# A fourth pair of weight tiles, another order of the seven steps, and other ranks in the feed-forward of a hybrid encoder

## The chip, the cores and the metric

The kernel runs on one core of a Trainium2 chip. The metric is the device time of one execution in microseconds (us). A core has five engines that run side by side, each with its own stream of instructions in a fixed order: TensorE (PE in the profile; PEld is its weight load), VectorE (DVE), ScalarE (ACT), GpSimd (POOL) and SyncE (SP). An engine that waits at one instruction runs none of those behind it. [...]

## What is computed

544 tokens (512 of a new stream, 32 of a running one) go through two layers of width 1024. Around the mixers (Mamba-2 in layer 0, stick-breaking attention in layer 1) stand four SwiGLU feed-forwards of 2816 hidden columns, and these are what the change touches:

```python
def swiglu(h, w_gate, w_up, w_down):
    return (jax.nn.silu(h @ w_gate) * (h @ w_up)) @ w_down
...
x = x + 0.5 * swiglu(rms_norm(x, ffn_norm[i, 0]), ffn_w_gate[i, 0], ffn_w_up[i, 0], ffn_w_down[i, 0])
...        # mixer
x = x + 0.5 * swiglu(rms_norm(x, ffn_norm[i, 1]), ffn_w_gate[i, 1], ffn_w_up[i, 1], ffn_w_down[i, 1])
```

## The kernel before

The stream x lies transposed in the core's memory, 1024 features as 8 blocks c of 128 partitions, with all T = 544 tokens as columns; H = 272 is half of them. Every product is made of three matmuls in a rounded format: a value is taken apart into a high part and the rest (`xh`, `xl` for data, `whi`, `wlo` for weights), and hi·hi, hi·lo and lo·hi are added. So each weight tile that arrives by DMA must be converted before PE can use it: `whi<-...` on ACT or POOL, then `wlo<-...` on DVE or POOL (`halve`). The converted pairs are the scarce store: `NW = 3` pairs in turn, and the conversion for the step after next can only start when PE has left a pair.

One feed-forward (class `Sevens`, called four times, FF0 to FF3 below) runs its 22 blocks f of 128 hidden columns so:

- f = 0 to 3 are plain: gate and up product, 8 blocks c each (`product`).
- The other 18 go as nine pairs, x0 to x8, each by a Strassen-Winograd scheme of seven steps (`STEPS`): a11, s3, s2, a12, s1, a22, s4. Here a11, a12, a22 are quarters of the weight matrix, s3 and s1 are sums of two quarters, s2 is s3 plus a22, and s4 is s2 plus a12. A step is 24 matmuls of 272 columns on one weight pair. Sums of x's parts (`xfh`, `xfl`) are made once per feed-forward.
- The hidden values of a group of pairs are multiplied by the down weights by the same seven steps, twice per group (for two halves of the outputs): h0 and h0' after x1, h1 and h1' after x4, h2 and h2' after x7. A step is 18 matmuls, on `h3h`/`h4h` parts; its result is added to x by DVE (`add`: `x<-mm,x`). Four last products d0 to d3 close the feed-forward.

A sum such as s3 comes by two DMAs: SP fetches one quarter into the tile `s`, then POOL issues a second that adds the other quarter (`added`). There is one s3 tile: the next pair's s3 is fetched when the last one's is converted and s2 has been formed from it.

What sets the order of instructions on an engine is a planner (class `Plan`). Chains of work ask for time on an engine, for a slot ("get", "put") or for an event ("wait", "set"); each chain has a rank, and of those ready the lowest rank goes first. DMAs stand in it as fixed sleeps:

```python
            def added(self, key, tag, name):
                yield "sleep", 4.5
                yield "D", 1.0, lambda: G.dma_start(self.raw[key, tag][:, :self.width(key)], self.quarter_of(key, name), accum_op=ALU.add)
                yield "sleep", 5.0
                yield "set", ("raw", key, tag)
```

The conversions have rank 10, `add` and the copies of banks (`save`, `quarter`) 20, and `plain`, which turns the two banks of a plain f into hidden values, has the rank of the chain that starts it. The steps of x0 and of all h groups run in the order (0, 3, 2, 1, 4, 5, 6) of `STEPS`, those of x1 to x8 in the order 0 to 6. A plain f, and a pair's product, goes into one of four places in PSUM (`mm`), which PE can fill again only when ACT or DVE has read it.

Of the kernel before, what the change touches and what calls it, by code (L numbers as in the profile page):

```python
# [9 lines left out]
P = 128  # L10
# [171 lines left out]
def _body(tc, io):  # L182
# [22 lines left out]
    with ExitStack() as ctx:  # L205
# [3 lines left out]
        def halves(ap):  # L209
            return ap.rearrange("p (a b) -> p a b", a=2)  # L210

        xg = {}

# [138 lines left out]
        class Norm:  # L352
            def __init__(self, name, ring=None, share=None):
                self.g = NORMS[name]
                self.name = name
                self.ring = ring
                self.share = share
                self.parts = [None] * KC
                self.acc = None

            def ops(self, c):
                h, l = self.place(c)
                gp = gains[:, self.g, c:c + 1]
                yield "S", s_cost(T), lambda: S.activation(h, x[c], AF.Identity, scale=gp)
                yield "V", v_cost(T) + 0.06, lambda: V.scalar_tensor_tensor(out=l, in0=x[c], scalar=gp, in1=h.bitcast(F32), op0=ALU.mult, op1=ALU.subtract)
# [68 lines left out]
        def opening(norm, psum, tmp):  # L434
# [17 lines left out]
            def block(c):  # L452
                h, l = norm.place(c)
                gp = gains[:, norm.g, c:c + 1]
                S.activation(h, x[c], AF.Identity, scale=gp)
                V.scalar_tensor_tensor(out=l, in0=x[c], scalar=gp, in1=h.bitcast(F32), op0=ALU.mult, op1=ALU.subtract)

# [96 lines left out]
        STEPS = (("a11", "A", "b11"), ("s3", "D", 1), ("s2", "A", 2), ("a12", "B", "b21"), ("s1", "A", 0), ("a22", "D", 3), ("s4", "A", "b22"))  # L554

        class Sevens:

            NW = 3

            def __init__(self, plan, i, norm, bank, tmp, hidden, roles, after, first=(), opened=None, ahead=None, done=None):  # L560
# [5 lines left out]
                self.forms = Forms(norm)  # L566
                self.hs, self.hf, self.loaded, self.raw, self.gu = {}, {}, {}, {}, {}
# [62 lines left out]
            def weights(self):  # L630
                raw, tmp = self.raw, self.tmp
                for k, u in enumerate(self.units):
                    n, free = 1024, None
                    if k < len(self.first):
                        yield "get", "w"
                        self.loaded[k] = self.first[k]
                        yield "set", ("part", k)
                        continue
# [27 lines left out]

                    third = k % self.NW == 2
                    if third and k >= len(self.units) - self.NW:
                        yield "get", "w"
                        third = False  # L670
                    yield "get", "w"
                    if third:
                        hi, lo = (tmp.tile([P, 1024], F32R, tag=t, name=t) for t in ("whi", "wlo"))
                    else:
                        hi, lo = weight_parts()
                    self.loaded[k] = hi, lo
                    yield "spawn", self.halve(k, n, src, hi, lo, free), -2 if k == 0 and self.opened else 10
# [19 lines left out]
            def dense(self):  # L697
                banks = {}
                for k, u in enumerate(self.units):
# [3 lines left out]
                    if u[0] == "s":  # L703
# [16 lines left out]
                        for c in range(n):  # L720
# [31 lines left out]
                    elif u[0] == "p":  # L752
# [7 lines left out]
                        for c in range(KC - (late and j == 0)):  # L760
                            if late and j == 1 and c == 2:
                                yield "T", 0.753, lambda: product(banks[f, 0], self.loaded[k - 1], self.norm.parts, only=KC - 1)
                                yield "put", "w"
                                yield "set", "f0"
                            yield "T", 0.753, lambda: product(ps, self.loaded[k], self.norm.parts, only=c)
                        if not late or j == 1:
                            yield "put", "w"
                        if j == 1:
                            yield "spawn", self.plain(f, banks[f, 0], ps, self.plain_banks[f % 2])
                    else:  # L770
# [3 lines left out]
                        for at, (m, e) in enumerate(order):  # L774
# [7 lines left out]
                            if e == n - 1:  # L782
                                yield "spawn", self.leave(m, ps, f"b{b}"), 9
                        yield "put", "w"
# [94 lines left out]

            def united(self, p, u, w, s, t, *slots):  # L880

# [12 lines left out]
                yield "V", v_cost(H) + 0.06, lambda: V.scalar_tensor_tensor(out=s3, in0=s2, scalar=-1.0, in1=w0, op0=ALU.mult, op1=ALU.subtract)  # L894
                yield from self.apart(h3[:, 1:3, :], l3[:, 1:3, :], w, T)
                yield "set", ("hf", p, "b21")
                yield "set", ("hf", p, "b22")
# [7 lines left out]
            def plain(self, f, pg, pu, banks):  # L905
# [1347 lines left out]
```

## Time and profile before

| | |
|---|---|
| median of 3 runs | 2251.42 us (2250.7 to 2253.66) |
| profiled execution, its own time | 2249.7 us |
| its span, first to last instruction | 2247.8 us |
| granted TensorE clock | 0.995 of full speed |
| PE busy | 2204.1 us (98%), 17505 matmuls |
| DVE busy | 1827.7 us (81%), 2491 instructions |
| ACT busy | 1098.8 us (49%) |
| POOL busy | 597.6 us (27%) |
| DMA | 319 MB, 142 GB/s on average |

Stages, read from the timeline: FF0 to 380 us, Mamba to 804, FF1 to 1162, an embedding stage and the keys and values to 1250, FF2 to 1615, attention to 1806, FF3 to 2170, the rest to 2248. In the profile every operation has line 194, that of a recording helper, so groups are told apart by the names of their tiles. The duration of a POOL DMA row (0.9 us) is the issue alone; the landing is given by the DMA views.

### The profile page before, as it was taken

To read this page: it belongs to the slowest core of one execution; us is meant where nothing else is said; L and a number is where in the kernel's file an instruction comes from. 1 tells how busy PE (TensorE), PEld (TensorE's weight loads), DVE (VectorE), ACT (ScalarE), POOL (GpSimd) and SP (SyncE) were. 2 spreads that over 40 slices of the span, in tenths; PEclk is the share of its full clock that TensorE was granted. 3 is DMA by queue.
4 is the path that set the end of the run, shared out by engine and by line. 5 is a ranking of instruction groups with operands and counts; after the bars stand their busy time and mean duration, and the time that the engine had idled before them with its cause. 6 is when DMAs were issued, how large, how long until landed. Compare 5 with 4: busy or idle time off the path is not lost. (4 is left out here: it accounts for less than half of the span.)

```text
span 2247.8 us, 42746 instructions
## 1 busy us (share of the span) xinstructions
PE 2204.1 (98%) x17505; PEld 2152.0 (96%) x17505; DVE 1827.7 (81%) x2491; ACT 1098.8 (49%) x1585; POOL 597.6 (27%) x622
## 2 busy tenths in 40 slices
PE   9999999999999999999999999999998999999997
PEld 9999999999999999999999999999986899999997
DVE  7889887778877688898867788988788688898867
ACT  5434434567746454344345443443557254344353
POOL 2221321254323112222210223222234322222204
PEclk9999999999999999999999999999999999999999
DMA  6576862332333255868632658686311156868622
GB/s 211 139 205 165 218 161 76 113 113 92 108 108 95 92 160 140 216 167 207 160 94 85 200 141 209 171 208 159 100 47 49 53 167 148 214 167 202 158 86 78
DMA packets 117955, 319.23 MB, mean 142 GB/s; under 512 B 15200, under 2 KB 36320, under 8 KB 117760
## 3 DMA queue, kind: packets, MB, share of 16 engines
q1 hardware_dynamic: 91760, 233.23, 32.1%
q0 software_dynamic: 23120, 77.74, 19.3%
q10 hardware_dynamic: 2880, 5.53, 0.7%
q8 instruction: 138, 2.26, 0.4%
q14 instruction: 57, 0.47, 0.1%
HBM read 309.75 MB, written 6.71 MB: 141 GB/s over the span
## 5 line engine op out<-in xcount | busy, mean ns | idle before, releaser
L194 PE MATMUL mm<-xh,whi 128*128 128x272 f32 x2096 | 512.9, 292 | 5.8 <-DVE sq L194 3.8
L194 PE MATMUL mm<-xl,whi 128*128 128x272 f32 x2096 | 506.4, 289 | 0.3 <-DVE xl L194 0.3
L194 PE MATMUL mm<-xh,wlo 128*128 128x272 f32 x2096 | 505.1, 289 | 0.5 <-DVE wlo L194 0.5
L194 ACT ACTIVATE whi<-s 128x1024 fp32r<-128x1024 f32 (+1 forms) x196 | 190.5, 972 | 409.5 <-PE mm L194 291.8
L194 PEld LDWEIGHTS mm<-xh,whi 128*128 128x128 f32 x2096 | 357.0, 188 | 16.5 <-issue 13.9
L194 PEld LDWEIGHTS mm<-xh,wlo 128*128 128x128 f32 x2096 | 357.6, 189 | 0.7 <-DVE wlo L194 0.7
L194 PEld LDWEIGHTS mm<-xl,whi 128*128 128x128 f32 x2096 | 357.2, 189 | 0.5 <-DVE xl L194 0.5
L194 PE MATMUL mm<-xfh,wlo 128*128 128x272 f32 x1152 | 333.0, 289 | 9.3 <-DVE wlo L194 9.3
L194 PE MATMUL mm<-xfh,whi 128*128 128x272 f32 x1152 | 332.6, 289 | 1.0 <-ACT whi L194 0.9
L194 PE MATMUL mm<-xfl,whi 128*128 128x272 f32 x1152 | 331.7, 288 | 0.0
L194 DVE TENSOR_TENSOR wlo<-s,whi 128x1024 fp32r<-128x1024 f32 (+1 forms) x240 | 275.4, 1148 | 37.8 <-ACT whi L194 26.1
L194 ACT ACTIVATE whi<-a 128x1024 fp32r<-128x1024 f32 (+1 forms) x154 | 152.6, 991 | 221.0 <-PE mm L194 165.8
L194 DVE TENSOR_TENSOR wlo<-wraw,whi 128x1024 fp32r<-128x1024 f32 (+2 forms) x146 | 181.9, 1247 | 62.1 <-ACT whi L194 44.6
L194 DVE TENSOR_TENSOR wlo<-a,whi 128x1024 fp32r<-128x1024 f32 (+1 forms) x181 | 204.0, 1127 | 30.2 <-ACT whi L194 22.6
L194 PEld LDWEIGHTS mm<-xfh,wlo 128*128 128x128 f32 x1152 | 216.6, 188 | 12.0 <-DVE wlo L194 12.0
L194 PE MATMUL mm<-h4h,wlo 128*128 128x272 f32 x832 | 219.3, 289 | 1.8 <-DVE wlo L194 1.8
L194 PE MATMUL mm<-h4h,whi 128*128 128x272 f32 x832 | 219.3, 289 | 1.6 <-DVE x L194 1.5
L194 PEld LDWEIGHTS mm<-xfh,whi 128*128 128x128 f32 x1152 | 216.6, 188 | 2.6 <-ACT whi L194 2.3
L194 PE MATMUL mm<-h4l,whi 128*128 128x272 f32 x832 | 218.9, 288 | 0.0
L194 PEld LDWEIGHTS mm<-xfl,whi 128*128 128x128 f32 x1152 | 216.7, 188 | 0.0
L194 ACT ACTIVATE whi<-wraw 128x1024 fp32r<-128x1024 f32 (+2 forms) x116 | 119.8, 1034 | 172.9 <-PE mm L194 105.2
L194 POOL DMA_DIRECT2D s<-in_wgq x108 | 95.1, 881 | 353.7 <-DMA s<-in_wgq 146.4
(322 smaller groups left out, 4982.6 us busy)
## 6 DMA issues: line engine op xcount, KB each, us to landing
a<-in_wgq SPq DMA_DIRECT2D x108, 512.0 KB, 5.9
s<-in_wgq POOLq DMA_DIRECT2D x108, 512.0 KB, 7.4
s<-in_wgq SPq DMA_DIRECT2D x72, 512.0 KB, 4.4
a<-in_wd SPq DMA_DIRECT2D x72, 384.0 KB, 4.5
wraw<-in_win SPq DMA_DIRECT2D x41, 512.0 KB, 3.6
s<-in_wd SPq DMA_DIRECT2D x48, 384.0 KB, 3.1
s<-in_wd POOLq DMA_DIRECT2D x48, 384.0 KB, 7.3
wraw<-in_wgu SPq DMA_DIRECT2D x29, 512.0 KB, 3.7
```

The costliest lines, as they stand in the source:

```text
L194: ins = getattr(self.engine, op)(*args, **kw)
```

## The change

1. **Fourth weight pair.** x's parts for c < 4 now lie in two tiles of [128, 2, 4, 272] (class `Apart`), so that half 1 of all four, which only the plain products read, is one piece of 1088 columns. After the last plain product it serves as a fourth pair, until the last step of x8. It has the name of the part it lies in, so a conversion into it reads `xh<-...` and `xl<-...` in the rows. Pairs are handed out in the order in which PE leaves them. The writes of these parts are now 128x2x272 in form, formerly 128x544.
2. **Order of steps.** In x1 to x8, a22 is now the fourth step and a12 the sixth. The second half of each hidden group (h0', h1', h2') takes s3 as its second step (formerly the fourth), and a22 as its fourth.
3. **Ranks.** `add` goes from 20 to 9, ahead of the conversions; `plain` gets 4; a slot of the last plain pair is freed earlier.

```diff
+        class Apart:
+            def __init__(self, tile, c):
+                self.whole = tile[:, :, c, :]
+
+            def __getitem__(self, key):
+                a, start = divmod(key[1].start, H)
+                return self.whole[:, a, start:start + key[1].stop - key[1].start]
...
-                yield "S", s_cost(T), lambda: S.activation(h, x[c], AF.Identity, scale=gp)
+                yield "S", s_cost(T), lambda: S.activation(whole(h), halves(x[c]), AF.Identity, scale=gp)
...
-                    self.parts[c] = tuple(xg["pool"].tile([P, T], F32R, tag=f"x{k}{c}", name=f"x{k}{c}") for k in "hl")
+                    if c < 4 and not self.near:
+                        self.near = [xg["pool"].tile([P, 2, 4, H], F32R, tag=f"x{k}", name=f"x{k}") for k in "hl"]
+                    self.parts[c] = tuple(Apart(v, c) for v in self.near) if c < 4 else \
+                        tuple(xg["pool"].tile([P, T], F32R, tag=f"x{k}{c}", name=f"x{k}{c}") for k in "hl")
...
+        LATE, SOON = (0, 3, 2, 1, 4, 5, 6), (0, 1, 2, 5, 4, 3, 6)
...
+                self.places = ["pool", "pool", "tmp"]
...
-                    self.units += [("s", ("x", p), s) for s in ((0, 3, 2, 1, 4, 5, 6) if p == 0 else range(7))]
+                    self.units += [("s", ("x", p), s) for s in (LATE if p == 0 else SOON)]
...
-                            self.units += [("s", ("h", g, a), s) for a in range(2) for s in (0, 3, 2, 1, 4, 5, 6)]
+                            self.units += [("s", ("h", g, a), s) for a in range(2) for s in (SOON if a else LATE)]
...
-                    third = k % self.NW == 2
-                    if third and k >= len(self.units) - self.NW:
+                    yield "get", "w"
+                    place = self.places.pop(0)
+                    while place == "tmp" and k >= len(self.units) - self.NW or place == "x" and k > self.last_step:
                         yield "get", "w"
-                        third = False
-                    yield "get", "w"
-                    if third:
+                        place = self.places.pop(0)
+                    if place == "tmp":
                         hi, lo = (tmp.tile([P, 1024], F32R, tag=t, name=t) for t in ("whi", "wlo"))
+                    elif place == "x":
+                        hi, lo = (v[:, 1, :, :].rearrange("p c n -> p (c n)")[:, :1024] for v in self.norm.near)
...
-                        yield "put", "w"
+                        yield from self.leave_w(k)
                         if hidden:
-                            yield "spawn", self.add(it, s, ps, f"b{b}" if s in (3, 5, 6) else None), 20
+                            yield "spawn", self.add(it, s, ps, f"b{b}" if s in (3, 5, 6) else None), 9
...
+                        if (f, j) == (NPLAIN - 1, 1):
+                            self.places.append("x")
                             yield "put", "w"
                         if j == 1:
-                            yield "spawn", self.plain(f, banks[f, 0], ps, self.plain_banks[f % 2])
+                            yield "spawn", self.plain(f, banks[f, 0], ps, self.plain_banks[f % 2]), 4
...
+            def leave_w(self, k):
+                self.places.append(self.placed[k])
+                yield "put", "w"
...
-                    yield from self.united(f // 2, a, b, s, t, "sq", "acc")
-                    yield "put", "sq"
-                    yield "put", "c2"
+                    yield from self.united(f // 2, a, b, s, t, "sq", "acc", early=("c2", "sq"))
```

The planner then writes another order for the whole program. PE has as many matmuls as before, SP as many DMAs. POOL multiplies gate by up (`gu<-gu`) 6 times instead of 24, DVE does the rest, and POOL makes 10 of the `wlo` instead of 1.

**Place 1: h1' and x5 in FF1.** DVE before, from the conversion of h1' a11 on; `s3_11679` is the s3 of h1', `s3_11859` that of x5, `x2_67<-mm` an addition to x:

```order
L194 TENSOR_TENSOR wlo_11762<-a11_11584,whi_11761 128x768
L194 SCALAR_TENSOR_TENSOR x2_67<-mm_11709,x2_67 128x2x272
L194 TENSOR_TENSOR wlo_11787<-a12_11724,whi_11786 128x768
L194 TENSOR_TENSOR s2_11803<-s3_11679,a22_11744 128x768
L194 SCALAR_TENSOR_TENSOR x0_65<-mm_11629,x0_65 128x2x272
L194 TENSOR_TENSOR wlo_11819<-s2_11803,whi_11818 128x768
L194 SCALAR_TENSOR_TENSOR x1_66<-mm_11811,x1_66 128x2x272
L194 TENSOR_TENSOR wlo_11836<-s3_11679,whi_11835 128x768
```

DVE now, from the same conversion on; `s3_11573` is the s3 of h1':

```order
L194 TENSOR_TENSOR wlo_11643<-a11_11459,whi_11642 128x768
L194 SCALAR_TENSOR_TENSOR x2_67<-mm_11537,x2_67 128x2x272
L194 TENSOR_TENSOR s2_11690<-s3_11573,a22_11622 128x768
L194 SCALAR_TENSOR_TENSOR x2_67<-mm_11614,x2_67 128x2x272
L194 TENSOR_TENSOR wlo_11689<-s3_11573,whi_11688 128x768
L194 SCALAR_TENSOR_TENSOR x0_65<-mm_11537,x0_65 128x2x272
L194 TENSOR_TENSOR wlo_11707<-s2_11690,whi_11706 128x768
```

The last use of the s3 tile of h1' (the conversion `wlo<-s3`) has moved ahead of that of s2 and by one addition to x; the conversion of a12 has gone behind it.

ACT now, in x5; `c0`, `c3` and `c1` are the copies of PE's results of a11, s3 and s2 out of PSUM, `xh_9123<-s1` is a conversion into the fourth pair:

```order
L194 ACTIVATE xh_9123<-s1_11775 128x1024
L194 ACTIVATE c0_11940<-mm_11896 128x544
L194 ACTIVATE whi_11969<-a12_11816 128x1024
L194 ACTIVATE h3h_11905<-gu1_11511 128x544
L194 ACTIVATE c3_11977<-mm_11933 128x544
L194 ACTIVATE c1_12011<-mm_11896 128x544
```

ACT before, in x5:

```order
L194 ACTIVATE whi_12027<-a12_11903 128x1024
L194 ACTIVATE c0_12036<-mm_11989 128x544
L194 ACTIVATE whi_12064<-s1_11884 128x1024
L194 ACTIVATE c3_12072<-mm_12029 128x544
L194 ACTIVATE h3h_11998<-gu1_11604 128x544
L194 ACTIVATE whi_12101<-a22_11923 128x1024
```

The copy `c3` now stands behind a conversion and an `h3h`; the step a22, which goes into the same place in PSUM, now follows s3 with one step between, formerly with three.

**Place 2: the plain blocks of FF0.** DVE before, up to the reading of the banks of f = 2 (`sq_736<-mm_465` and `sq_737<-mm_534`):

```order
L194 TENSOR_TENSOR s2_671<-s3_295,a22_297 128x1024
L194 TENSOR_TENSOR wlo_670<-a12_322,whi_669 128x1024
L194 TENSOR_TENSOR xfl3_288<-gu1_651,xfh3_284 128x1088
L194 TENSOR_TENSOR h4l_549<-sq_407,h4h_548 128x544
L194 TENSOR_TENSOR h4l_549<-acc_472,h4h_548 128x544
L194 TENSOR_TENSOR sq_736<-mm_465,r_360 128x544
L194 TENSOR_TENSOR wlo_733<-s2_671,whi_732 128x1024
L194 TENSOR_TENSOR sq_737<-mm_534,r_360 128x544
```

DVE now, up to the same two (`sq_663<-mm_461` and `sq_664<-mm_528`) and on to the conversions:

```order
L194 TENSOR_TENSOR wlo_598<-a11_287,whi_597 128x1024
L194 TENSOR_TENSOR xfl2_281<-gu1_581,xfh2_277 128x1088
L194 TENSOR_TENSOR gu1_650<-gu0_616 128x544
L194 TENSOR_TENSOR sq_663<-mm_461,r_354 128x544
L194 TENSOR_TENSOR h4l_514<-acc_457,h4h_513 128x544
L194 SCALAR_TENSOR_TENSOR gu1_650<-gu1_650,gu0_616 128x272
L194 TENSOR_TENSOR sq_664<-mm_528,r_354 128x544
L194 SCALAR_TENSOR_TENSOR gu1_650<-gu1_650,gu0_616 128x272
L194 TENSOR_TENSOR xfl3_282<-gu1_650,xfh3_278 128x1088
L194 TENSOR_TENSOR s2_669<-s3_289,a22_291 128x1024
L194 TENSOR_TENSOR acc_730<-mm_599,r_354 128x544
L194 TENSOR_TENSOR wlo_668<-a12_316,whi_667 128x1024
```

The reading of f = 2's first bank has moved ahead of the total for s2, of the conversion of a12, of `xfl3` and of both `h4l`.

**Place 3: the additions to x in h0 of FF1.** DVE before:

```order
L194 SCALAR_TENSOR_TENSOR x0_65<-mm_10518,x0_65 128x2x272
L194 TENSOR_TENSOR wlo_10544<-s3_10281,whi_10543 128x768
L194 SCALAR_TENSOR_TENSOR x0_65<-mm_10545,x0_65 128x2x272
L194 TENSOR_TENSOR wlo_10568<-s1_10372,whi_10567 128x768
L194 TENSOR_TENSOR s2_10485<-s2_10485,a12_10332 128x768
L194 TENSOR_TENSOR wlo_10595<-a22_10409,whi_10594 128x768
L194 SCALAR_TENSOR_TENSOR x2_67<-mm_10518,x2_67 128x2x272
```

DVE now:

```order
L194 SCALAR_TENSOR_TENSOR x0_65<-mm_10443,x0_65 128x2x272
L194 TENSOR_TENSOR wlo_10472<-s1_10264,whi_10471 128x768
L194 TENSOR_TENSOR gu0_10426<-gu0_10426 128x544
L194 SCALAR_TENSOR_TENSOR x0_65<-mm_10473,x0_65 128x2x272
L194 TENSOR_TENSOR s2_10374<-s2_10374,a12_10302 128x768
L194 TENSOR_TENSOR xl_9124<-a22_10230,xh_9123 128x768
L194 SCALAR_TENSOR_TENSOR x2_67<-mm_10443,x2_67 128x2x272
```

Between the last two additions one conversion fewer stands now; the total and the conversion of a22 still do. The multiplication `gu0<-gu0` has come to DVE from POOL.

More of the change, by code (lines that the diff above doesn't have):

```diff
@@ L210, in halves, with whole @@
             return ap.rearrange("p (a b) -> p a b", a=2)
+        class Apart:
[4 more added lines that the diff above has]
+                return self.whole[:, a, start:start + key[1].stop - key[1].start]
+        def whole(v):
+            return v.whole if isinstance(v, Apart) else halves(v[:, :])
         xg = {}
@@ L359, in __init__ @@
                 self.acc = None
+                self.near = None
             def ops(self, c):
@@ L363, in ops @@
                 gp = gains[:, self.g, c:c + 1]
-                yield "S", s_cost(T), lambda: S.activation(h, x[c], AF.Identity, scale=gp)
-                yield "V", v_cost(T) + 0.06, lambda: V.scalar_tensor_tensor(out=l, in0=x[c], scalar=gp, in1=h.bitcast(F32), op0=ALU.mult, op1=ALU.subtract)
+                yield "S", s_cost(T), lambda: S.activation(whole(h), halves(x[c]), AF.Identity, scale=gp)
+                yield "V", v_cost(T) + 0.06, lambda: V.scalar_tensor_tensor(out=whole(l), in0=halves(x[c]), scalar=gp, in1=whole(h).bitcast(F32), op0=ALU.mult, op1=ALU.subtract)
                 if self.share is None:
@@ L454, in block @@
                 gp = gains[:, norm.g, c:c + 1]
-                S.activation(h, x[c], AF.Identity, scale=gp)
-                V.scalar_tensor_tensor(out=l, in0=x[c], scalar=gp, in1=h.bitcast(F32), op0=ALU.mult, op1=ALU.subtract)
+                S.activation(whole(h), halves(x[c]), AF.Identity, scale=gp)
+                V.scalar_tensor_tensor(out=whole(l), in0=halves(x[c]), scalar=gp, in1=whole(h).bitcast(F32), op0=ALU.mult, op1=ALU.subtract)
             def times(j, c):
@@ L566, in __init__ @@
                 self.forms = Forms(norm)
-                self.hs, self.hf, self.loaded, self.raw, self.gu = {}, {}, {}, {}, {}
+                self.hs, self.hf, self.loaded, self.raw, self.gu, self.placed = {}, {}, {}, {}, {}, {}
+                self.places = ["pool", "pool", "tmp"]
                 self.units, self.loads = [], []
@@ L635, in weights @@
                         yield "get", "w"
+                        self.placed[k] = self.places.pop(0)
                         self.loaded[k] = self.first[k]
@@ L762, in dense @@
                                 yield "T", 0.753, lambda: product(banks[f, 0], self.loaded[k - 1], self.norm.parts, only=KC - 1)
-                                yield "put", "w"
+                                yield from self.leave_w(k - 1)
                                 yield "set", "f0"
@@ L766, in dense @@
                         if not late or j == 1:
+                            yield from self.leave_w(k)
+                        if (f, j) == (NPLAIN - 1, 1):
+                            self.places.append("x")
                             yield "put", "w"
                         if j == 1:
-                            yield "spawn", self.plain(f, banks[f, 0], ps, self.plain_banks[f % 2])
+                            yield "spawn", self.plain(f, banks[f, 0], ps, self.plain_banks[f % 2]), 4
                     else:
@@ L783, in dense @@
                                 yield "spawn", self.leave(m, ps, f"b{b}"), 9
-                        yield "put", "w"
+                        yield from self.leave_w(k)
                         if q == 3:
@@ L878, in outcome, with united @@
                     yield "set", ("h", f)
-            def united(self, p, u, w, s, t, *slots):
+            def united(self, p, u, w, s, t, *slots, early=()):
                 yield "get", "F4"
@@ L895, in united @@
                 yield from self.apart(h3[:, 1:3, :], l3[:, 1:3, :], w, T)
+                for slot in early:
+                    yield "put", slot
                 yield "set", ("hf", p, "b21")
```

1 line of the change is left out of this document (added).

## Prediction

> **What bounds the kernel now.** I read the page first: busy times, then the groups of instructions with the idle time ahead of them.
>
> ```profile
> span 2247.8 us, 42746 instructions
> PE 2204.1 (98%) x17505; PEld 2152.0 (96%) x17505; DVE 1827.7 (81%) x2491; ACT 1098.8 (49%) x1585; POOL 597.6 (27%) x622
> ...
> L194 PE MATMUL mm<-xh,whi 128*128 128x272 f32 x2096 | 512.9, 292 | 5.8 <-DVE sq L194 3.8
> L194 PE MATMUL mm<-xfh,wlo 128*128 128x272 f32 x1152 | 333.0, 289 | 9.3 <-DVE wlo L194 9.3
> L194 PE MATMUL mm<-xfh,whi 128*128 128x272 f32 x1152 | 332.6, 289 | 1.0 <-ACT whi L194 0.9
> L194 PE MATMUL mm<-h4h,wlo 128*128 128x272 f32 x832 | 219.3, 289 | 1.8 <-DVE wlo L194 1.8
> L194 PE MATMUL mm<-h4h,whi 128*128 128x272 f32 x832 | 219.3, 289 | 1.6 <-DVE x L194 1.5
> ```
>
> PE is busy for 2204.1 of 2247.8 us, so 43.7 us is all that any reordering can win, and the matmuls themselves are not touched. The right column tells what PE waited for: 9.3 us for a `wlo` on the x pairs' sums, 0.9 for a `whi` there, 3.8 for DVE's reading of a bank (`sq`), 1.5 for an addition to x. The timeline of PE puts the first two (10.2 us) at twelve places, each the step s3 of the x pair that follows h0', h1' or h2'. I take x5 in FF1 as the pattern and read the timeline of five engines; then the DMAs issued there, each from issue to landing.
>
> ```profile
> 1006.24 0.95 DVE L194 TENSOR_TENSOR wlo<-s,whi 128x768 fp32r<-128x768 f32 x1
> 1007.22 0.33 SPq L614 DMA_DIRECT2D s<-in_wgq  x1
> 1011.35 0.89 POOL L194 DMA_DIRECT2D s<-in_wgq  x1 [0.51 <-DMA s<-in_wgq]
> 1020.65 1.06 ACT L194 ACTIVATE whi<-s 128x1024 fp32r<-128x1024 f32 x1 [5.34 <-DMA s<-in_wgq]
> 1021.77 1.22 DVE L194 TENSOR_TENSOR wlo<-s,whi 128x1024 fp32r<-128x1024 f32 x1
> 1021.77 0.40 PE L194 MATMUL mm<-xfh,whi 128*128 128x272 f32 x1
> 1023.04 0.39 PE L194 MATMUL mm<-xfh,wlo 128*128 128x272 f32 x1 [0.76 <-DVE wlo L194]
> ```
>
> ```profile
> s<-in_wgq SPq DMA_DIRECT2D x1, 512.0 KB, 3.6
> s<-in_wgq POOLq DMA_DIRECT2D x1, 512.0 KB, 9.2
> ```
>
> The chain reads: the s3 of h1' is converted as that group's fourth step, ending at 1007.19; SP refills the tile at once (3.6 us), POOL adds the second quarter (9.2 us), then come `whi` 1.06 and `wlo` 1.22. 1007.2 to 1023.0 is 15.8 us, and PE wants the result 0.76 us sooner. Between x pairs the same chain has 21 us (seven steps of 3.0), which is why only the pair after a short h' waits.
>
> The length of a step I take from a stretch without gaps:
>
> ```profile
> 250.00:300.00 50.00, 50.00 (x402) 50.00 (x401) 46.01 (x58) 24.91 (x33) 11.85 (x13) 1.00 0.75 189
> ```
>
> 402 matmuls in 50 us is 0.124 each: 3.0 us for an x step (24), 2.25 for an h step (18), 0.75 for one block c of a product (6).
>
> **The s3 waits, 10.2 us.** Now s3 is the second step of h' (place 1). Its own supply:
>
> ```profile
> 991.22 2.63 SPq L614 DMA_DIRECT2D s<-in_wd  x2
> 994.94 0.91 POOL L194 DMA_DIRECT2D s<-in_wd  x1 [4.72 <-DMA s<-in_wd]
> 1002.72 0.96 DVE L194 TENSOR_TENSOR s<-s,a 128x768 f32<-128x768 f32 x1 [0.23 <-DMA a<-in_wd]
> ...
> s<-in_wd POOLq DMA_DIRECT2D x1, 384.0 KB, 5.6
> a<-in_wd SPq DMA_DIRECT2D x1, 384.0 KB, 6.7
> ```
>
> The summed s3 lands at 994.94 + 5.6 = 1000.5. DVE's order is then total, one addition to x, `wlo`: 0.96 + 0.72 + 0.96, so about 1003.2 to 1003.5. The total also needs a22, which landed only at 1002.6 (6.7 us after its issue at 995.9, behind a12's); SP now issues it ahead of a12, some 1.5 us sooner, so about 1001. The step's first `wlo` matmul is due near 1005.4 (x5's s3 begins at 1021.77; less its a11, 3.0, and six steps of h1', 13.5, is 1005.3), so there is 1.9 us in hand. The tile is free 3.7 us sooner than 1007.2. By the same durations x5's s3 is whole at 1003.5 + 3.6 + 0.6 + 9.2 = 1016.9 and converted at 1019.3, against a need at 1022.3: 3 us in hand. Price: the whole 10.2 us, twelve times. If x5's second DMA takes 12.2 (the longest in the row that sums up all DMAs into `s`, below) the wait is 0.2, not 0.76, so at least 7 of the 10.2 go as long as h1' itself isn't late. POOL has a `wlo` of a22 ahead of that issue, which is new; POOL stood idle 4.72 us there, and that covers it.
>
> [...]
>
> **FF0's bank, 3.8 us.** DVE and PE ahead of the only long gap in a feed-forward:
>
> ```profile
> 51.67 1.29 DVE L194 TENSOR_TENSOR xfl<-gu,xfh 128x1088 fp32r<-128x1088 f32 x1 [0.39 <-ACT xfh L194]
> ...
> 53.23 1.89 DVE L194 TENSOR_TENSOR gu<-gu 128x544 f32<-128x544 f32 x1
> ...
> 57.45 1.22 DVE L194 TENSOR_TENSOR wlo<-a,whi 128x1024 fp32r<-128x1024 f32 x1
> 58.58 1.28 DVE L194 TENSOR_TENSOR xfl<-gu,xfh 128x1088 fp32r<-128x1088 f32 x1
> ...
> 61.05 0.71 DVE L194 TENSOR_TENSOR sq<-mm,r 128x544 f32<-128x544 f32 x1
> 61.91 0.56 PE L194 MATMUL mm<-xh,whi 128*128 128x272 f32 x1 [3.83 <-DVE sq L194]
> ```
>
> PE stands from 58.1, waiting for `sq<-mm` at 61.05. Now (place 2) that read comes right after `xfl2` and one `gu`. Even if `xfl2` starts no sooner than 51.67 and `gu` takes the 1.89 seen, it ends by 51.67 + 1.29 + 1.89 + 0.71 = 55.6, 2.5 us before PE asks. What is late next is the `wlo` of a12, put back: from 55.6 there are `h4l` 0.71, `gu` 0.44, `sq` 0.71, `gu` 0.44, `xfl` 1.28, total 1.22, `acc` 0.71 and itself 1.22, so 62.3 at worst against 61.3 (58.1 + 3.0 and two matmuls). With the rows that the new order clears ahead of `xfl2` the read comes nearer 52 and the `wlo` nearer 59. So −2.8 to −3.8; I take −3.8.
>
> **The additions to x, 1.5 us.** Two places, 0.75 each (FF1 and FF3, h0):
>
> ```profile
> 892.79 0.72 DVE L194 SCALAR_TENSOR_TENSOR x<-mm,x 128x544 f32<-128x544 f32 x1
> 893.59 2.10 DVE L194 TENSOR_TENSOR wlo<-s,whi 128x768 fp32r<-128x768 f32 x1
> 893.53 3.38 POOL L194 TENSOR_TENSOR gu<-gu 128x544 f32<-128x544 f32 x2
> 900.25 0.36 PE L194 MATMUL mm<-h4h,whi 128*128 128x272 f32 x1 [0.75 <-DVE x L194]
> ```
>
> By place 3, from 892.79: 0.72, `wlo` 0.95, `gu` 0.72, x 0.72, total 0.95, `wlo` 0.95, x 0.72 end at 898.5, before PE's 899.5. With the 2.10 seen for `wlo` beside POOL's `gu<-gu` it would be 899.7, a wait of 0.2. −1.1 to −1.5; I take −1.5, since that POOL work is gone. [...]
>
> **Added.** (a) a22 as fourth step must wait for ACT's copy `c3` of s3, one step of 3.0 us earlier, 32 pairs. Ahead of the copy stand at most a conversion (1.06) and an `h3h` (0.65); with the copy's 0.61 and some 0.25 of handover 2.6 of 3.0 us: hidden by 0.4, costs nothing while ACT isn't behind.
>
> ```profile
> 1026.97 0.61 ACT L194 ACTIVATE c<-mm 128x544 f32<-128x544 f32 x1
> 1027.48 0.65 ACT L194 ACTIVATE h3h<-gu 128x544 fp32r<-128x544 f32 x1
> ```
>
> (b) x's parts c < 4 are one tile, so at the entrance of FF2 the first write waits for all of the keys' reads of it:
>
> ```profile
> 1243.05 6.01 ACT L194 ACTIVATE xh<-x,gains 128x544 fp32r<-128x544 f32 x8
> 1249.27 0.73 PE L194 MATMUL mm<-ident,kv 128*128 128x128 f32 x4 [0.34 <-DVE kv L194]
> ```
>
> The product before that transpose ends at 1248.3, so its c = 3 at 1245.3; four writes of 0.75 end at 1248.3, DVE's `xl` and `kv` behind them at 1249.8 instead of 1249.2: +0.6. (c) 128x2x272 forms: the additions to x have two pieces as well and take 0.72 where the contiguous `sq<-mm` takes 0.71: four writes in the opening, +0.1 with both engines. (d) 18 `gu<-gu` come to DVE (13 us) and nine conversions leave it (11 us); DVE is at 81%, no sum. (e) The d steps' 1.8 us (`h4h,wlo`) have the same rows ahead of them and stay.
>
> **Sum:** −10.2 − 3.8 − 1.5 + 0.7 = −14.8 against the profiled execution's 2249.7: 2234.9. The median of the runs stands 1.7 above it, so 2236.6; I say 2237.
>
> **Rivals.**
> 1. *Part of the s3 gain comes back at h' step 2.* There the chain has 1.9 us with a landing of 5.6. At 9.2, which the next such DMA took, it is 1.7 late. The page's medians speak for something between:
>
> ```profile
> s<-in_wgq POOLq DMA_DIRECT2D x108, 512.0 KB, 7.4
> ...
> s<-in_wd POOLq DMA_DIRECT2D x48, 384.0 KB, 7.3
> ...
> DMA to landing us min/median/max: 2.7/5.5/12.2
> ```
>
> 7.3 still fits (0.2 in hand). If half of the twelve land at 9.2: 6 x 1.7 = 10, so 2247; with a third, 2243.
> 2. *Slower by the same mechanism.* If all twelve land at 9.2 or later, 12 x 1.7 = 20 and the time is 2257; it decides from 8.8 us on, where 12 x 1.2 eats the 14.8. Against it: POOL's issue there isn't moved later, and 5.6 was measured at this very place.
> 3. *Slower by ACT:* one more conversion ahead of `c3` makes a22 0.6 late, 32 x 0.6 = 20: 2256. It decides from 0.45 per pair. Against it: ACT is at 49%.
> 4. *The change doesn't bring s3 sooner* (SP's refill held by the DMA ahead of it): only 3.8 + 1.5 − 0.7 go, 2247.
>
> **Chances.** The forecast 0.60, its own range 2232 (the d waits gone too, or the opening better) to 2242 (rows at their worse ends: 7 + 2.8 + 1.1 − 0.7). Rival 1 0.18, rival 4 0.10, rivals 2 and 3 0.08 together, 0.04 for nothing measurable. 0.2%, 4.5 us, is about what a measurement can tell from no change. Faster: the forecast, two thirds of 1 and half of 4, 0.77; slower 0.09; same 0.14. Range 2232 to 2250, up to rivals 1 and 4.
>
> **What would show it.** In the groups: `xfh,wlo` idle from 9.3 to under 1, `xh,whi <-DVE sq` without its 3.8, `h4h,whi <-DVE x` near 0; `ident,kv` near 0.9; PE's busy time unchanged. Wrong would be: a wait of `h4h,wlo` or `h4h,whi` for DVE or ACT at second steps of h', or a wait of `xfh,whi` for ACT's `c`.

## The result and the profile after

The changed kernel's median is 2233.7 us (2231.76 to 2234.42, 4 runs) beside 2251.06 us for the kernel before in the same runs: ratio 0.992, 95% interval 0.9903 to 0.9937. The profiled execution took 2233.66 us, 16.0 us less than the one profiled before. A further series on another chip gave 2234.86 us and 0.9939 (0.9925 to 0.9952).

The page of the changed kernel, the rows that answer to those of the prediction; busy times, then PE's groups with the idle time ahead of them:

```profile
span 2232.0 us, 42746 instructions
PE 2197.8 (98%) x17505; PEld 2149.5 (96%) x17505; DVE 1807.5 (81%) x2493; ACT 1090.2 (49%) x1573; POOL 621.9 (28%) x632
...
L194 PE MATMUL mm<-xh,whi 128*128 128x272 f32 x1872 | 448.2, 293 | 2.6 <-ACT xh L194 0.9
L194 PE MATMUL mm<-xh,wlo 128*128 128x272 f32 x1872 | 440.5, 289 | 3.3 <-DVE wlo L194 3.3
...
L194 PE MATMUL mm<-xfh,whi 128*128 128x272 f32 x864 | 249.3, 289 | 0.8 <-ACT c L194 0.8
L194 PE MATMUL mm<-xfh,wlo 128*128 128x272 f32 x864 | 248.9, 288 | 0.0
L194 PE MATMUL mm<-h4h,wlo 128*128 128x272 f32 x688 | 177.5, 288 | 3.1 <-DVE wlo L194 3.1
L194 PE MATMUL mm<-h4h,whi 128*128 128x272 f32 x688 | 177.7, 289 | 1.4 <-DVE x L194 1.3
```

`xfh,wlo` had 9.3 us of idle time and has none: all twelve s3 waits are gone. `xh,whi` lost its 3.8 us for `sq`, but `xh,wlo` has 3.3 us where it had 0.5. `h4h,wlo` went from 1.8 to 3.1, and `h4h,whi` still has 1.3, now at another place. The groups count fewer matmuls since those on the fourth pair are listed under its own name (`mm<-xfh,xh`, for instance).

The chain at x5 of FF1, timelines of five engines and the landing of the DMAs; the reader should follow the s3 tile:

```profile
988.63 0.87 POOL L194 DMA_DIRECT2D s<-in_wd  x1
994.76 0.96 DVE L194 TENSOR_TENSOR s<-s,a 128x768 f32<-128x768 f32 x1 [1.20 <-issue]
996.27 1.27 DVE L194 TENSOR_TENSOR wlo<-s,whi 128x768 fp32r<-128x768 f32 x1
997.57 0.33 SPq L634 DMA_DIRECT2D s<-in_wgq  x1
1001.58 0.88 POOL L194 DMA_DIRECT2D s<-in_wgq  x1 [4.84 <-DVE wlo L194]
1010.90 1.22 DVE L194 TENSOR_TENSOR wlo<-s,whi 128x1024 fp32r<-128x1024 f32 x1
1015.82 0.29 PE L194 MATMUL mm<-xfh,whi 128*128 128x272 f32 x1
...
s<-in_wd POOLq DMA_DIRECT2D x1, 384.0 KB, 6.1
...
s<-in_wgq POOLq DMA_DIRECT2D x1, 512.0 KB, 8.1
```

The sum for h1' landed at 994.7; its `wlo` ended at 997.5 and SP refilled the tile at 997.57. h1' needed that `wlo` near 999.6 (1015.82 less 3.0 and six steps of 2.25, and two matmuls), so 2.0 us were in hand where the prediction had 1.9. x5's own s3 was converted at 1012.1 and wanted at 1016.1: 4 us, forecast 3.

**A ledger by starts.** PE runs the same number of matmuls in both kernels, and step follows step with the same sizes, so the start of the n-th matmul after can be held against the n-th before. The difference grows or shrinks only where one kernel waits, or runs its matmuls slowly, and the other doesn't. This is what "by starts" means below. Between the two profiled executions it gives:

| place | forecast, us | by starts, us |
|---|---|---|
| twelve s3 waits | −10.2 | −13.7 |
| FF0: bank of f = 2, and the a12 conversion behind it | −3.8 | −0.9 |
| two additions to x in h0 (FF1, FF3) | −1.5 | −2.1 |
| opening | +0.1 | +1.25 |
| entrance of FF2 | +0.6 | +0.4 |
| addition to x in h0 of FF0 | 0 | +1.45 |
| d steps of FF1 | 0 | +1.2 |
| end of FF0 (a wait of 0.77 for a square) | 0 | −1.1 |
| the rest, no place over 0.85 | 0 | −2.6 |
| sum | −14.8 | −16.1 |

### The profile page after: what moved, and what is told of

Its sections match the earlier page's. It is cut to its first block, busy times and chain, and to the rows that moved or that the text cites. A ratio compares the mean times of both kernels' runs of the same rounds, so it can differ in the third digit from the quotient of the medians.

```text
span 2232.0 us, 42746 instructions
## 1 busy us (share of the span) xinstructions
PE 2197.8 (98%) x17505; PEld 2149.5 (96%) x17505; DVE 1807.5 (81%) x2493; ACT 1090.2 (49%) x1573; POOL 621.9 (28%) x632
## 4 chain that ended last, share of the span: by engine, by line
PE 85%; DVE 6%; DMA 3%; ACT 2%; issue 2%; POOL 0%; SPq 0%; DVEq 0%; ACTq 0%; POOLq 0%
PE mm L194 75%; PE z L194 4%; PE aux L194 3%; DMA s<-in_wgq 1%; PE f L194 1%; PE tr L194 1%; PE o L194 1%; DVE wlo L194 1%; DVE x L194 1%; ACT whi L194 1%; DMA wraw<-in_wgu 0%; DVE xl L194 0%; DMA plr<-in_p 0%; DVE gu L194 0%; DVE fu L194 0%
## 5 line engine op out<-in xcount | busy, mean ns | idle before, releaser
L194 PE MATMUL mm<-xh,whi 128*128 128x272 f32 x1872 | 448.2, 293 | 2.6 <-ACT xh L194 0.9
L194 PE MATMUL mm<-xh,wlo 128*128 128x272 f32 x1872 | 440.5, 289 | 3.3 <-DVE wlo L194 3.3
L194 PE MATMUL mm<-xl,whi 128*128 128x272 f32 x1872 | 441.3, 289 | 0.3 <-DVE xl L194 0.3
L194 ACT ACTIVATE whi<-s 128x1024 fp32r<-128x1024 f32 (+1 forms) x135 | 131.1, 971 | 256.8 <-PE mm L194 133.8
L194 PE MATMUL mm<-xfh,whi 128*128 128x272 f32 x864 | 249.3, 289 | 0.8 <-ACT c L194 0.8
L194 PE MATMUL mm<-xfh,wlo 128*128 128x272 f32 x864 | 248.9, 288 | 0.0
L194 PE MATMUL mm<-xfl,whi 128*128 128x272 f32 x864 | 248.9, 288 | 0.0
L194 DVE TENSOR_TENSOR wlo<-s,whi 128x1024 fp32r<-128x1024 f32 (+1 forms) x180 | 208.2, 1157 | 29.1 <-ACT whi L194 18.7
L194 DVE SCALAR_TENSOR_TENSOR x<-mm,x 128x544 f32<-128x544 f32 x200 | 143.5, 718 | 24.9 <-PE mm L194 24.2
L194 PEld LDWEIGHTS mm<-xfl,whi 128*128 128x128 f32 x864 | 162.6, 188 | 0.0
```

The source lines that it names most:

```text
L194: ins = getattr(self.engine, op)(*args, **kw)
```

## The experiments

Eight kernels undo or do parts of the change (one of them with another landing time in the planner), three move ranks on top of it (one with another landing time too), and one is the changed kernel again. Ratios are to the kernel before on the same chip.

**Only h' in the old order.**

```diff
-  self.units += [("s", ("h", g, a), s) for a in range(2) for s in (SOON if a else LATE)]
+  self.units += [("s", ("h", g, a), s) for a in range(2) for s in LATE]
```

> The changed kernel with one thing undone: h0', h1', h2' run their steps in the old order again (s3 fourth). Theory S (the s3 waits went because s3 of h' is converted two steps sooner and its tile is refilled sooner): the twelve waits of xfh,wlo for DVE wlo come back, about 9 us of idle time in the group, and by the starts of the matmuls 11 to 14 us, so 2245 to 2248 us. Rival W (the fourth weight pair lets conversions run ahead, the order does nothing): no such waits, 2234 us. Rival R (the ranks did it): 2234 us as well.

2276.37 us, 1.0141 (1.0124 to 1.0158): a loss of more than three times what theory S priced, so the order in h' is needed, but not only for the s3 waits: of the twelve only three stand in this kernel (3.1 us), which theory S did not expect. PE waited 26.8 us for ACT's copies `c`, in 17 places, and 4.3 us for `wlo`. Neither W nor R fits either.

**Only the order in h'**, on the kernel before.

```diff
-  ... for a in range(2) for s in (0, 3, 2, 1, 4, 5, 6)]
+  ... for a in range(2) for s in ((0, 1, 2, 5, 4, 3, 6) if a else (0, 3, 2, 1, 4, 5, 6))]
```

> The kernel before with one thing done: h0', h1', h2' run in the new order. Theory S: the xfh,wlo group loses nearly all of its 9.3 us of idle time and the time falls by 11 to 14 us, to 2237 to 2240 us; the wait of 3.8 us for sq in FF0 and the two of 0.75 us for x stay. Rival W: the waits stay, 2251 us; or they move to step s3 of h' itself, since with three pairs the conversion of s3 there cannot start earlier.

2248.82 us, 1.0003 (0.9991 to 1.0016). No gain, although the mechanism works, as PE's groups of this kernel show:

```profile
L194 PE MATMUL mm<-xfh,wlo 128*128 128x272 f32 x1152 | 331.8, 288 | 0.0
L194 PE MATMUL mm<-h4h,whi 128*128 128x272 f32 x832 | 220.5, 290 | 8.4 <-DVE x L194 8.2
L194 PE MATMUL mm<-h4h,wlo 128*128 128x272 f32 x832 | 220.9, 291 | 5.6 <-POOL wlo L194 3.7
```

The s3 waits are at zero (14.9 us won by starts), and in their stead PE waits 8.4 us for additions to x, most of them in the first halves h0 to h2, and 5.6 us for conversions in h' and d. The wait for `sq` in FF0 is longer too (4.4 us). The profiled execution, 2253.33 us, was the slowest of the twelve. The first half of theory S holds, its time does not.

**Without the fourth pair.**

```diff
-  if (f, j) == (NPLAIN - 1, 1):
-      self.places.append("x")
-      yield "put", "w"
```

> The changed kernel without the fourth weight pair (x's parts still lie in the two tiles, the orders and ranks are the new ones). Theory S: s3 waits stay gone; what three pairs can lose is a conversion that now comes one step later, at most small waits of wlo or whi in h' and for the copy before a22: 2234 to 2239 us. Rival W: 10 to 14 us come back, 2244 to 2248 us.

2252.62 us, 1.0015 (1.0002 to 1.0028). The s3 waits are gone here too; the time is even worse than rival W's, and it came by another way, the prediction's first rival. PE's groups, then step 2 of h1' in FF1 from the second DMA of its s3 on, and that DMA's landing:

```profile
L194 PE MATMUL mm<-xfh,wlo 128*128 128x272 f32 x1152 | 332.0, 288 | 0.0
L194 PE MATMUL mm<-h4h,wlo 128*128 128x272 f32 x832 | 221.2, 291 | 14.0 <-POOL wlo L194 9.3
994.35 0.91 POOL L194 DMA_DIRECT2D s<-in_wd  x1 [4.47 <-DMA s<-in_wd]
1002.37 0.85 ACT L194 ACTIVATE whi<-s 128x768 fp32r<-128x768 f32 x1 [4.79 <-DMA s<-in_wd]
1003.30 1.81 POOL L194 TENSOR_TENSOR wlo<-s,whi 128x768 fp32r<-128x768 f32 x1 [5.79 <-ACT whi L194]
1005.16 0.40 PE L194 MATMUL mm<-h4h,wlo 128*128 128x272 f32 x1 [1.33 <-POOL wlo L194]
...
s<-in_wd POOLq DMA_DIRECT2D x1, 384.0 KB, 7.9
```

ACT starts the conversion as the sum lands, at 1002.3, only 1.6 us before PE needs the `wlo` (1003.8), and the planner gave the `wlo` to POOL, where it takes 1.81 instead of 0.95. In the changed kernel the same DMA was issued 10.9 us ahead of PE's need instead of 9.5 (SP's fetch before it starts when the conversion of h1's s3 frees the tile, and that came sooner) and landed in 6.1 us instead of 7.9. Over the twelve places the sum of h' lands 4.7 to 7.2 us ahead of the need in the changed kernel and 1.5 to 4.3 us ahead with three pairs. 14.0 us of idle time at step 2 of h' and in d take the place of the s3 waits (15.0 us by starts here). So the fourth pair is what makes room for the earlier step; why the landing is shorter with it is not shown.

**x1 to x8 in the old order.**

```diff
-  ... for s in (LATE if p == 0 else SOON)]
+  ... for s in (LATE if p == 0 else range(7))]
```

> The changed kernel with x1 to x8 in the old order of steps (a12 fourth, a22 sixth). Theory S: the s3 waits stay gone, the two waits of 0.4 us for ACT's copy c vanish, the rest within 2 us: 2232 to 2236 us. Rival (a22 as fourth step frees the a22 tile sooner, and that brings the totals s2 and so s3 sooner): waits of xfh for wlo of s2 or s3 come back, 2238 us or more.

2238.71 us, 0.9953 (0.9935 to 0.9971). The s3 waits stay gone; two waits for ACT's copy stay (0.9 us), against the expectation. What is new is that PE waits for additions to x in 8 places (5.0 us), against 2 (2.1 us) in the changed kernel and 4 (3.3 us) in its second profile. The median is the rival's, but the rival named another wait, so neither theory had it right. By the ratios a22 as fourth step would be worth 0.1 to 0.3%, but the intervals overlap with those of the changed kernel, so that it gains anything is not shown.

**All steps in the old orders**, with the fourth pair and the ranks of the change (both edits above).

> The changed kernel with all steps in the old orders (x1 to x8 with a12 fourth, all of h with s3 fourth); the fourth pair and the ranks stay. It splits the loss of the run with only h' in the old order (1.014 of before) into the late s3 itself and what a late s3 does when a22 is the fourth step of x. Theory P (a late s3 holds DVE at its total; the multiplications behind it come late, ACT waits for them, and ACT's copy c3 stands behind them; with a22 as the fourth step PE needs that copy three steps sooner): the 26.8 us of waits for ACT c are gone, the s3 waits are there (9 to 13 us), and the time is that of before less what the ranks bring, 2243 to 2250 us, ratio 0.997 to 1.001. Rival (the fourth pair itself does harm when s3 comes late): still 1.01 or more.

2280.22 us, 1.0133 (1.0116 to 1.0151). Theory P is wrong: 25.1 us of waits for ACT's copies stand without a22 as the fourth step. Of the twelve s3 waits eight are back (7.4 us), as the forecast's mechanism asks. What the copies wait for shows in this kernel in FF1 after h0'; the last line is the landing of the DMA in the first:

```profile
933.92 0.88 POOL L194 DMA_DIRECT2D s<-in_wgq  x1 [3.37 <-ACT c L194]
942.84 1.06 ACT L194 ACTIVATE whi<-s 128x1024 fp32r<-128x1024 f32 x1 [4.73 <-DMA s<-in_wgq]
943.80 0.60 ACT L194 ACTIVATE c<-mm 128x544 f32<-128x544 f32 x1
944.46 0.59 PE L194 MATMUL mm<-xfh,whi 128*128 128x272 f32 x1 [3.75 <-ACT c L194]
...
s<-in_wgq POOLq DMA_DIRECT2D x1, 512.0 KB, 8.8
```

ACT stands at a conversion whose data is still under way, and the copy behind it, for which PE waits from 940.7 on, could not start. The conversion is that of s4 of the same pair: its DMA is issued at 933.92, just after the `wlo` of s2 (933.39), and no fetch by SP stands before it, as one would for an s3 or s1. PE needs s4 only two steps later. The planner reckons 5.0 us for that landing, which took 8.8. Eight of the 19 waits, 20.3 of the 25.1 us, stand behind a conversion of s4 in this way, with landings of 7.2 to 8.8 us. So the rival's time holds: the fourth pair and the ranks without the new orders do harm. That the fourth pair is what lets the planner put s4 ahead of the copy is argued, not shown.

**The same, with the planner's landing time at 7.4 us.**

```diff
   yield "D", 1.0, lambda: G.dma_start(..., accum_op=ALU.add)
-  yield "sleep", 5.0
+  yield "sleep", 7.4
   yield "set", ("raw", key, tag)
```

> All steps in the old orders with fourth pair and new ranks (2280 us, 25.1 us of waits for ACT's copies c), and one number changed: the planner reckons 7.4 us, not 5.0, from POOL's issue of an adding DMA to its landing, which is the median measured (7.1 to 7.4). Theory Q (the fourth pair lets the planner put the conversion of s3 ahead of the copies c on ACT, because it believes s3 landed; ACT then stands at that conversion, 4.7 us at 942.8 us, with the copy behind it that PE needs): the waits for ACT c fall from 25 to under 8 us and the time by 15 us or more, to 2250 to 2265 us. Rival (a late s3 holds ACT in any order, because the conversion is due before the copies): within 8 us of 2280.

2283.32 us, 1.0159 (1.0143 to 1.0175). The waits for copies fell from 25.1 to 17.8 us, and as much came up elsewhere (10.0 for `wlo`, 5.2 each for x and for DVE's `c`). But the edit changes the landing of s3 and s1 only; that of s4, behind which the copies stood, has a number of its own (in `fourth`) and stays at 5.0. So this run is no test of what held ACT in the run above, and that number at 7.4 was not tried with these orders. In the new plan the eight places are gone, and nearly all copies that PE waits for stand behind a `gu<-gu` of ACT that waits for DVE.

**Additions to x at rank 20.**

```diff
-  yield "spawn", self.add(it, s, ps, f"b{b}" if s in (3, 5, 6) else None), 9
+  yield "spawn", self.add(it, s, ps, f"b{b}" if s in (3, 5, 6) else None), 20
```

> The changed kernel with the additions to x at rank 20 again. In the run with the new order in h' and nothing else, 11 waits of PE for DVE's x stood, 9.0 us in all. Theory: these are what rank 9 takes away, so they come back here: 8 to 12 us, 2241 to 2246 us. Rival (the fourth pair took them away, since the conversions that stood ahead of the additions now come earlier): at most 2 us, 2234 to 2236 us.

2288.81 us, 1.0182 (1.0164 to 1.0201), some 55 us slower than the changed kernel. The waits of PE and DVE in h0 of FF0:

```profile
PE mm L194 <- DVE x L194: 46.5, 22, 4.7
...
106.88 0.95 DVE L194 TENSOR_TENSOR wlo<-s,whi 128x768 fp32r<-128x768 f32 x1
107.75 0.94 DVE L194 TENSOR_TENSOR s<-s,a 128x768 f32<-128x768 f32 x1
108.61 1.54 DVE L194 SCALAR_TENSOR_TENSOR x<-mm,x 128x544 f32<-128x544 f32 x2
109.47 0.56 PE L194 MATMUL mm<-h4h,whi 128*128 128x272 f32 x1 [4.29 <-DVE x L194]
```

Right in kind, short by a factor of five in size: with four pairs more conversions are ready at any time, and at rank 10 they go ahead of every addition at rank 20. Rank 9 is not one of three gains but what the rest of the change needs. That it is the pair and not the orders that needs it is argued from the run with the order in h' alone, which has three pairs and rank 20 and 9.0 us of these waits.

**`plain` at its old rank.**

```diff
-  yield "spawn", self.plain(f, banks[f, 0], ps, self.plain_banks[f % 2]), 4
+  yield "spawn", self.plain(f, banks[f, 0], ps, self.plain_banks[f % 2])
```

> The changed kernel with the rank of plain inherited (20) again. By the ledger of the starts of PE's matmuls the place in FF0 is worth only 0.9 us net in the change: 5.2 us won at the bank of f = 2 (a wait of 3.8 us and slow matmuls behind it), 4.3 lost at the conversion of a12 that was put back. So theory: within 2 us of the changed kernel, 2233 to 2236 us, the wait for sq of some 4 us back and the one of 2.8 us for wlo gone. Rival (the forecast's price): 3.8 us slower, 2237 to 2238 us.

2236.2 us, 0.9943 (0.993 to 0.9955); the profiled execution took 2233.95, that of the changed kernel 2233.66. The wait for `sq` in FF0 is back (2.8 us, where 4 were expected), the one for a12 gone, and some copies are late (4.1 us). The old rank costs 0.3 us by the profiled executions, 2.5 by the medians and 1 to 5 by the ratios to the two series of the changed kernel, so the theory and the rival are not told apart.

**Conversions of d first.**

```diff
-  yield "spawn", self.halve(k, n, src, hi, lo, free), -2 if k == 0 and self.opened else 10
+  yield "spawn", self.halve(...), -2 if k == 0 and self.opened else 1 if u[0] == "d" else 10
```

> The changed kernel with rank 1 for the conversions of d0 to d3 alone. The 2.27 us wait of h4h,wlo in FF1 and the 0.80 in FF3 fall to under 0.3 each; by the starts of the matmuls 2 to 3 us won: 2230 to 2232 us beside 2233.7. Rival (nl and x that were passed are late next, for the next norm): 2233 to 2235 us.

2224.71 us, 0.9899 (0.9885 to 0.9913), against 0.9939 (0.9925 to 0.9952) for the changed kernel on the same chip: the fastest of all, and 5 us better than expected. Its profiled execution took 2228.04 us beside 2233.75 there. By starts 2.4 us are won in FF1's d steps, about 1.5 from FF3's d steps to the end; the medians differ by more (10 us) than the profiled executions (5.7; this one was the slowest of its four), and what lies between is not explained.

**d first, the last sum of x's parts late.**

```diff
-  yield "spawn", self.halve(c, s)
+  yield "spawn", self.halve(c, s), 11 if c == 3 else 5
```

> The changed kernel with two ranks altered: the taking apart of the last sum of x's parts (xfh3, xfl3) gets 11, behind the conversions, and the conversions of d0 to d3 get 1. If the wait of 2.81 us for the a12 conversion in FF0 (and the slow matmuls behind it, 1.4 us) comes from xfl3 (1.29) and one reading of a bank (0.72) standing ahead of it, it falls to under 1 us: 3 to 4 us won. If the 2.27 us in FF1's d steps come from nl, x and acc ahead of the conversion, 1.5 to 2.2 us are won there. Together 2228 to 2231 us. Rival (the conversions then hold the next norm's or s2's work and the waits only move): 2233 us or more.

2231.29 us, 0.9923 (0.991 to 0.9937), with the edit of d above included. The waits for a12 in FF0 and for d are gone as forecast, and a new one of 5.4 us stands in FF0. ACT and PE:

```profile
77.18 1.06 ACT L194 ACTIVATE whi<-s 128x1024 fp32r<-128x1024 f32 x1 [7.68 <-DMA s<-in_wgq]
79.63 0.60 ACT L194 ACTIVATE c<-mm 128x544 f32<-128x544 f32 x1
80.29 0.60 PE L194 MATMUL mm<-xfh,whi 128*128 128x272 f32 x1 [5.40 <-ACT c L194]
```

PE came sooner, the DMA for x0's s4 did not (8.4 us from its issue at 68.67), and the copy stands behind that conversion: the wait moved by 12 us along the program.

**The same, with s4's landing at 6.5 us in the plan**, which puts that copy ahead.

```diff
-  yield "sleep", 5.0
+  yield "sleep", 6.5
```

> The changed kernel with three things: rank 11 for the taking apart of the last sum of x's parts, rank 1 for the conversions of d, and 6.5 us instead of 5.0 for the landing of the DMA that makes s4. In the run with the first two, ACT stood 7.7 us at the conversion of s4 in FF0 with the copy c3 behind it, and PE 5.4 us for that copy, though it needed s4 itself only a step of 3.0 us later. Now c3 stands ahead of it. Expected: of the 5.4 us some 3 to 4 go, of the matmuls running slowly behind it another 1; 2226 to 2229 us, ratio 0.989 to 0.991 of before. Rival (s4 is itself the bound there, or other places lose by the new order): 2230 us or more.

2231.3 us, 0.9924 (0.9911 to 0.9937). The 5.4 us wait is gone, two of 2.3 and 2.9 us stand a few steps further on (at 78.5 and 87.1 us). The first is for another copy behind the same conversion, whose DMA again took 8.4 us; the second is for a copy of DVE's, behind conversions and a total. So what is won in FF0 by letting PE run ahead is given back a few steps later, in part to the landing of s4.

**The changed kernel again.**

> The changed kernel itself, unaltered, for a comparison on the same chip: 0.990 to 0.994 of before.

2234.86 us, 0.9939 (0.9925 to 0.9952). Its profile has the a12 wait in FF0 at 1.49 us instead of 2.81, and the FF0 term at −3.45 instead of −0.9. The run with d first, whose instructions are the same up to FF1's d steps, has 1.61 and −3.6 there. That place differs between executions of one kernel; the last section has the granted clock there in two of them.

## Why the prediction was right

The time (2233.7, forecast 2237, range 2232 to 2250) and the direction are as forecast, and the main mechanism is shown: with the order of h' alone all twelve s3 waits go, and with the old orders eight of them come back. Term by term:

- **The s3 waits.** Right in mechanism: tile released sooner, landings of 6.1 and 8.1 us where the prediction took 5.6 and 9.2, slack at h1' step 2 of 2.0 us for 1.9. The term was too small, −10.2 for −13.7, since it was read as idle time. PE before, in x5:

```profile
1021.55 0.29 PE L194 MATMUL mm<-xh,wlo 128*128 128x272 f32 x1
...
1023.40 0.29 PE L194 MATMUL mm<-xfl,whi 128*128 128x272 f32 x1
```

  Five starts apart lie 1.85 us, where 0.62 would do: 1.2 us lost, with 0.76 in the column of idle time. A matmul is listed as busy for 0.29 us and the next starts 0.125 after it, so the long stop hides some 0.16 us in the row ahead of it, and the three starts next to it come 0.1 late each.
- **Why it needed all of the change.** The prediction priced the fourth pair at nothing and the rank of `add` at 1.5 us. The runs show that the earlier s3 alone gains 0, that the orders and ranks without the fourth pair lose 0.15%, and that everything but the rank of `add` loses 1.8%. Its rival 1, a late s3 at step 2 of h', is what the kernel with three pairs does, and it names the cause, a landing of 7.9 us and not 5.6. The forecast did not see that the fourth pair keeps it away, since it read its 5.6 us and the 1.9 us of slack from a kernel with three pairs and took them over; that they held here was in part luck.
- **FF0's bank.** This step was wrong, and its size came out as forecast in some executions only. The bound "even if `xfl2` starts no sooner than 51.67" was no bound: DVE of the changed kernel has the conversion of a11 ahead of it and starts it at 54.20:

```profile
52.87 1.22 DVE L194 TENSOR_TENSOR wlo<-a,whi 128x1024 fp32r<-128x1024 f32 x1
...
54.20 1.29 DVE L194 TENSOR_TENSOR xfl<-gu,xfh 128x1088 fp32r<-128x1088 f32 x1
...
57.23 0.71 DVE L194 TENSOR_TENSOR sq<-mm,r 128x544 f32<-128x544 f32 x1
...
61.09 1.29 DVE L194 TENSOR_TENSOR xfl<-gu,xfh 128x1088 fp32r<-128x1088 f32 x1 [1.18 <-ACT xfh L194]
...
64.07 1.22 DVE L194 TENSOR_TENSOR wlo<-a,whi 128x1024 fp32r<-128x1024 f32 x1
65.34 0.39 PE L194 MATMUL mm<-xh,wlo 128*128 128x272 f32 x1 [2.81 <-DVE wlo L194]
```

  The read at 57.2 still came before PE needed it. What was named as late next, the `wlo` of a12, had `xfl3` ahead of it, for which DVE waited 1.18 us; it ended at 65.3 and not at 62.3, and cost 2.81 us and slow matmuls behind it: −0.9 net for −3.8. In two further executions DVE reached it about 1.1 us sooner, the stop was 1.49 and 1.61 us with no slow matmuls behind it, and the term −3.45 and −3.6.
- **Additions to x.** Both waits went; 2.1 us by starts for 1.5, by the same mis-reading as above. One came new, in h0 of FF0 (1.28 us), where DVE has no gap from 104 us on: the additions were priced at two places and not looked for elsewhere.
- **Costs.** The entrance of FF2 was right (+0.4 for +0.6, its row has 0.72 for the forecast 0.9). The copy ahead of a22 costs 0.8 us in two of 32 places: hidden, as said. The d steps "have the same rows ahead of them and stay" was wrong: the rows are the same, but their order is not. `pll`, for which DVE waits 2.39 us for ACT, now stands ahead of two additions and one `nl` which DVE did before it in the old order, and the 1.08 us in FF1 became 2.27; the run with rank 1 for these conversions takes it away.
- **The opening**, +1.25 for +0.1. The writes of 128x2x272 take 0.75 us as before; PE ran slowly over another stretch: from 8 to 12 us the granted clock was 0.57, against 1.00 before and 1.00 with `plain` at its old rank. Runs with the same tiles differ in this term (+1.25, +1.5, but −0.6 with `plain` at its old rank), so it isn't the form; why the clock fell there in one and not in the other is open.

The sum came out close because errors offset each other: too small were s3 by 3.5 us, x by 0.6 and what was not forecast by 3.7 (FF0's end and the rest); too good were the FF0 bank by 2.9 and the costs by 3.6. The difference is the 1.3 us between −14.8 and −16.1. The other 1.7 us between 2237 and 2233.7 were added to bring the profiled execution to the median; in the changed kernel the two are the same.

## What to carry to other kernels

Price a wait by the starts of PE's matmuls around it, not by its idle time: here the difference was a third. A buffer more, an order that supplies earlier and a rank that lets the consumer through can be worth nothing or a loss when one of them is missing and 0.7% together, so test them in pairs before dropping one. In an engine's fixed order, never put work that waits for a DMA ahead of a copy that frees what the bottleneck needs next: here 20.3 us of PE's waits stood behind such work with all steps in the old orders, and 5.4 with the last sum of x's parts late. And when a run is to test a number in a plan, make sure first which tile the engine stood at: here the number for s3 was changed while ACT stood at s4.

## What the runs showed of the hardware

A stop of PE cost 1.3 and 1.5 us more than its length where the granted clock fell afterwards. Windows of PE in FF0, before (a stop of 3.83 us from 58.1 on), after (2.81 us from 62.5 on) and in the second profile of the changed kernel (1.49 us from 62.8 on); the third number from the end of a row, ahead of the DMA share and GB/s, is the granted clock:

```profile
61.00:65.00 4.00, 3.08 (x14) 3.12 (x15) 3.84 (x7) 1.32 (x2) 1.80 (x2) 0.57 0.24 60
```

```profile
64.00:68.00 4.00, 2.66 (x15) 2.66 (x16) 4.00 (x5) 3.94 (x6) 1.94 (x1) 0.79 0.39 106
68.00:72.00 4.00, 4.00 (x28) 4.00 (x28) 3.77 (x5) 0.00 (x0) 2.12 (x3) 0.78 0.64 114
```

```profile
64.00:68.00 4.00, 3.76 (x30) 3.76 (x30) 4.00 (x4) 2.84 (x5) 3.03 (x3) 1.00 0.44 135
68.00:72.00 4.00, 4.00 (x34) 4.00 (x33) 4.00 (x7) 0.62 (x1) 1.18 (x2) 1.00 0.84 142
```

Before, 13 matmuls after the stop start 0.226 us apart instead of 0.125 (1.3 us lost); after, six run at full speed and then 15 slowly (1.5 us); within both stretches the granted clock is 0.50. In the second profile none is slow, which is about half of the difference between −0.9 and −3.45. The length of the stop doesn't decide it alone: with all steps in the old orders a stop of 2.12 us (at 252.7 us) was followed by a granted clock of 0.72 over 4 us, one of 2.15 us (at 1404.9) by 1.00, and the 2.27 us in FF1's d steps by 1.00 as well. At the granted clock of 0.50 the starts lie a factor of 1.8 apart, 0.226 for 0.125. What decides whether a slow stretch follows a stop, and how soon, is not shown.
